# Block 1's attention on one Trainium2 core: a written TensorE order of head-set steps and dense pieces, key groups by turns, joined output banks

## The chip, the core and the metric

The kernel runs on one core of a Trainium2 chip. The metric is the device time of one execution in microseconds (us). TensorE (PE) multiplies; VectorE (DVE), ScalarE (ACT) and GpSimd (POOL) do the rest; SyncE (SP) issues most of the weight loads. A TensorE product is a weight load (PEld) and a matmul (PE).

## The reference, cut to what matters

Two blocks of two layers each, over 256 tokens of width 1024, all in float32. Block 1, the one whose attention changes:

```
for l in range(2):                                   # block 1
    p  = x @ w_in[l]                                 # split into NSA, MLA and forgetting-attention (FOX) parts
    o_nsa = nsa_attention(...)    # 8 heads of 64 in 2 key groups of 4 heads; three branches (compressed, selected, window)
    o_mla = mla_attention(...)    # 4 heads, key width 96
    o_fox = fox_attention(...)    # 4 heads, key width 64, decay added to the scores
    merged = sum(sigmoid(x @ w_gate)[i] * (o_i @ w_br_i)) ; y = merged @ w_out
    x = layer_norm(a * x + y)
    x = layer_norm(a * x + memory_cross_attention(x, mem))   # 4 heads of 64, 256 memory rows
    x = layer_norm(a * x + square(relu(x @ w_up)) @ w_down)
```

Every attention is `softmax(q k^T * scale + bias) v` for two blocks of 128 queries (t = 0 and 1; causal, so t = 0 sees 128 keys and t = 1 sees 256). Block 2 has pooling, retention and an RWKV-7 recurrence. The kernel computes that recurrence in two chunks of 128 tokens with the inverse of a unit triangular matrix per head.

## The kernel before, in words

**Dense products.** Each float32 weight is loaded by SP (`raw`), cast by ACT to a high part (`hi`, L112), and DVE subtracts to get the low part (`lo`, L113); a few units take POOL for L113 instead. A product is three matmuls (L138, L139, L140) with those parts. DVE and ACT therefore work through a queue of weight splits between all else they do, each in its fixed order. Small attention products are plain float32: one such instruction in the program shows as two in the trace.

**Order.** The Tile framework's scheduler orders each engine's instructions. Inside `tc.manual_schedule(engines={PE})` TensorE keeps the written order. Before, that is used in block 2's recurrence only, whose parts `yield` between pieces of dense products (`others`).

**Block 1's attention.** `scores` (L252) makes four heads' scores of one key group: matmuls at L263 into bank `s`, then the bias and the row maximum on DVE (L271) and the exponential on ACT (L274). NSA's group g = 0 has its keys and queries in rows 0 to 63 of `kvT` and `nqT`, g = 1 in rows 64 to 127; one call uses one half of the rows. `transposed` scales the weights by DVE and transposes them on TensorE (L295) into `PT`. `pv_pair` (L307) makes one pair of heads' outputs, 128x128, in a bank `o` of its own and splits it for the next product. `attend_nsa(t, g)` does both branches of one group; `attend_mla`, `attend_fox` and `attend_compressed` the rest. The scheduler lays these between the dense products of chunks 3 and 4 of `w_in` and of the gates (`gate_tanh`).

**Memory cross attention.** `Norm.finish` ends the layer norm (L338, L340 on DVE over `xr`, L343 the transposes), then come keys, query, `memory_scores`, `memory_values`, `memory_weights`, `attend_memory`, and the output product. The low parts of the key and query weights are made on POOL.

**Block 2's inverse.** The 16x16 diagonal blocks are inverted on DVE; the inverse and its transpose go to two DRAM scratch tensors, `zd` and `td`, on POOL's DMA queue (L1112, L1111) in pieces of 64 bytes, and come back block-diagonal as `TT` and `Tn` (L1122). `invert` starts with `Tn` (L1130). At the same time SP loads the weights of the retention part, on which ACT's cast and DVE's split, and behind them L1292 (`kT`) and the products L1339, depend.

Of the kernel before, what the change touches and what calls it, by code (L numbers as in the profile page):

```python
# [42 lines left out]
def program(ctx: ExitStack, tc: tile.TileContext, T: dict, out: bass.AP):  # L43
# [208 lines left out]
    def scores(nk, qk, addm):  # L252

        P = bt("P", [128, 4, 256], F32, 4)
        hb = 512 // nk
        sums = st("sums", [128, 4])
        nmx = st("nmx", [128, 4])
        for b in range(0, 4, hb):
            p = pst("s")
            pv = p[:, :hb * nk].rearrange("p (h k) -> p h k", k=nk)  # L260
            for i in range(hb):
                q, k = qk(b + i)
                pe.matmul(pv[:, i, :], lhsT=q, rhs=k, start=True, stop=True)  # L263
            if addm is None:
                src, sign = pv, 1.0
                ver.tensor_reduce(out=nmx[:, b:b + hb], in_=src, axis=AX.X, op=ALU.max, negate=True)
            else:
                src, sign = P[:, b:b + hb, :nk], -1.0
                am = addm(b, hb)
                for i in range(hb):  # L270
                    ver.tensor_tensor_reduce(out=src[:, i, :], in0=pv[:, i, :], in1=am[:, i, :], scale=-1.0,  # L271
                                             scalar=3e38, op0=ALU.add, op1=ALU.min, accum_out=nmx[:, b + i:b + i + 1])
            for i in range(hb):
                act.activation(out=P[:, b + i, :nk], in_=src[:, i, :], func=AF.Exp, bias=nmx[:, b + i:b + i + 1],  # L274
                               scale=sign, accum_out=sums[:, b + i:b + i + 1])
        return P, sums

# [8 lines left out]

    def transposed(P, sc, nk, tags=("t", "t")):

        res = []
        for kt in range(nk // 128):  # L290
            Pk = P[:, :, 128 * kt:128 * kt + 128]
            ver.tensor_mul(out=Pk, in0=Pk, in1=sc.unsqueeze(2).broadcast_to([128, 4, 128]))
            p = pst(tags[kt])
            for h in range(4):
                pe.transpose(p[:, 128 * h:128 * h + 128], Pk[:, h, :], ident)  # L295
            pt = bt("PT", [128, 4, 128], F32, 4)
            evac(pt.rearrange("p a b -> p (a b)"), p)
            res.append(pt)
        return res

    def pv_pair(dst, ki, t, terms):

        o = pst("o")
        both = list(zip(terms(0), terms(1)))
        for i, pair in enumerate(both):
            for half, (v, pt) in enumerate(pair):
                pe.matmul(o[64 * half:64 * half + 64, :128], lhsT=v, rhs=pt, start=i == 0, stop=i == len(both) - 1)  # L307
        h, l = dst.k(ki)
        s = slice(128 * t, 128 * t + 128)
        split_op(h[:, s], l[:, s], o[:, :128])  # L310

    class Norm:
# [18 lines left out]
        def finish(self, t):  # L331
            mv = st("mv", [128, 2])
            ver.bn_aggr(out=mv, in_=self.stats[t])
            r = rsqrt(mv[:, 1:2], LN_EPS)
            for i in range(2):
# [4 lines left out]
                ver.scalar_tensor_tensor(out=z, in0=z, scalar=r, in1=self.b[:, s], op0=ALU.mult, op1=ALU.add)  # L340
                p = pst("s" if self.op else ("s", "s", "t", "o")[2 * t + i])
# [38 lines left out]
    def block1_layer(l, x, xop, us, K):  # L380
# [210 lines left out]
        def attend_compressed(t):  # L591
# [17 lines left out]
            ver.tensor_mul(out=pcs, in0=pcs, in1=valid_c[:, t, :].unsqueeze(1).broadcast_to([128, 8, 16]))  # L609
            p = pst("t")  # L610
# [4 lines left out]
        def attend_nsa(t, g):  # L615
            nk = 128 * (t + 1)
            pts = []
            for br in range(2):
                kt_ = kvT[64 * g:64 * g + 64, 2 + br, 0:nk]
                b0 = 0 if t else 128  # L620
                P, sums = scores(nk, lambda h: (nqT[64 * g:64 * g + 64, h, tok(t)], kt_),
                                 lambda b, n: bias[:, 4 * g + b:4 * g + b + n, b0:b0 + nk])
                sc = st("sc", [128, 4])
                ver.reciprocal(out=sc, in_=sums)
                ver.tensor_mul(out=sc, in0=sc, in1=gates(t)[:, 4 * g:4 * g + 4, 1 + br])
                pts.append(transposed(P, sc, nk))

            for pr in range(2):
                def terms(half):
                    r = 2 * pr + half  # L630
                    res = [(vz[:, 4 * g + r, :], pct[t])]
                    for br in range(2):
                        for kt in range(t + 1):
                            res.append((vv[:, kt, 128 * br + 64 * g:128 * br + 64 * g + 64], pts[br][kt][:, r, :]))
                    return res
                pv_pair(oop, 2 * g + pr, t, terms)

        def attend(t, k0, qT, kT, vt, v0, kr):
            nk = 128 * (t + 1)
            tm = tri_bias[:, (0 if t else 128):256]  # L640
            P, sums = scores(nk, lambda h: (qT[0:kr, h, tok(t)], kT[0:kr, h, 0:nk]),
                             lambda b, n: tm.unsqueeze(1).broadcast_to([128, n, nk]))
            sc = st("sc", [128, 4])
            ver.reciprocal(out=sc, in_=sums)
            pt = transposed(P, sc, nk)
            for pr in range(2):
                pv_pair(oop, k0 + pr, t,
                        lambda half: [(vt[:, kt, v0 + 128 * pr + 64 * half:v0 + 128 * pr + 64 * half + 64],
                                       pt[kt][:, 2 * pr + half, :]) for kt in range(t + 1)])

        attend_mla = lambda t: attend(t, 4, mq, mk, mv, 0, 96)
        attend_fox = lambda t: attend(t, 6, fqT, fkT, vv, 256, 66)

        def gate_tanh(c, br):
            us = pairs(T["w_gate"][l], 8 * br + 4 * c)
            tt = bt("gt", [128, 4, 256], F32, 4)
            for j in range(0, 4, 2):
                p = pst("mm")
                for i in range(2):
                    gemm_b(p[:, 256 * i:256 * i + 256], xop, us, 128 * (j + i))  # L660
                act.activation(out=flat2(tt[:, j:j + 2, :]), in_=p, func=AF.Tanh, scale=0.5)
            return tt

        if first:
            turn()
        attend_mla(0)
        us = chunk(3)
        o = [pst("mm"), pst("mm")]
        gemm_a(o, xop, us)
        for t in range(2):  # L670
            evac(vv[:, t, :], o[t])
        attend_compressed(0)
        attend_mla(1)
        us = chunk_b(4)
        for j in range(4):
            p = pst("mm")
            gemm_b(p[:, 0:256], xop, us, 128 * j)
            for i in range(2):
                if j < 2:
                    act.activation(out=fqT[0:64, 2 * j + i, :], in_=p[64 * i:64 * i + 64, 0:256],  # L680
                                   func=AF.Copy, scale=0.125)
                else:
                    ver.tensor_copy(out=fkT[0:64, 2 * (j - 2) + i, :], in_=p[64 * i:64 * i + 64, 0:256])
        if x is None:
            x = load_x()
        th = {}
        attend_nsa(0, 0)
        th[0, 0] = gate_tanh(0, 0)
        attend_fox(0)
        attend_nsa(0, 1)  # L690
        attend_compressed(1)
        th[0, 1] = gate_tanh(0, 1)
        attend_nsa(1, 0)
        attend_fox(1)
        attend_nsa(1, 1)
        th[0, 2] = gate_tanh(0, 2)
        th[1, 0] = gate_tanh(1, 0)

        mop = new_op(8, "P", 4)
        for c in range(2):  # L700
            for br in range(3):
                if (c, br) not in th:
                    th[c, br] = gate_tanh(c, br)
# [30 lines left out]
        def memory_values():  # L734
            us = [unit(T["xa_kv"][l, 2 + i], 256, 4) for i in range(2)]
            o = [pst("mm"), pst("mm")]
            gemm_a(o, memop, us, n=256)
            for t in range(2):
                act.copy(out=xakv[:, 1, t], in_=o[t][:, :256])
# [7 lines left out]
        def memory_scores(t):  # L747
            return scores(256, lambda i: (xq[64 * (i // 2):64 * (i // 2) + 64, i % 2, tok(t)],
                                          xakv[64 * (i // 2):64 * (i // 2) + 64, 0, i % 2, :]), None)

        def memory_weights(P, sums):
            sc = st("sc", [128, 4])
            ver.reciprocal(out=sc, in_=sums)
            return transposed(P, sc, 256, ("s", "t"))

        def attend_memory(t, pt):
            for pr in range(2):
# [146 lines left out]
    def block2_layer(l, x, r, us, K, xop):  # L904
# [211 lines left out]
        def inverse_parts():  # L1116

            Tn = [bt("Tn", [128, 8, 64]) for n in range(2)]
            for n in range(2):
                for d, t in ((K["td"], Tn[n]), (K["zd"], TT[n])):  # L1120
                    for a in range(2):
                        pool.dma_start(out=t[half(a)], in_=flat(d, 16 + 8 * HS * n + 64 * 129 * a, [128, 64], [HS, 8], [1, 64]))  # L1122
# [685 lines left out]
```

## Time and profile before

| what | value |
|---|---|
| median of 3 runs | 1672.89 us (1668.97 to 1673.03) |
| profiled execution | 1675.49 us, its span 1673.6 us |
| TensorE busy | 95% of the span |
| DVE, ACT, POOL busy | 66%, 44%, 17% |
| granted TensorE clock, mean | 0.973 |

The span is the part of the execution that the trace covers; 1.9 us lie outside it. A TensorE row of the timeline shows start, duration and count; durations overlap the next instruction, so the price of a group is the distance to the start of the next row.

### The profile page before, as it was taken

To read this page: it belongs to the slowest core of one execution; us is meant where nothing else is said; L and a number is where in the kernel's file an instruction comes from. 1 tells how busy PE (TensorE), PEld (TensorE's weight loads), DVE (VectorE), ACT (ScalarE), POOL (GpSimd) and SP (SyncE) were. 2 spreads that over 40 slices of the span, in tenths; PEclk is the share of its full clock that TensorE was granted. 3 is DMA by queue.
4 is the path that set the end of the run, shared out by engine and by line. 5 is a ranking of instruction groups with operands and counts; after the bars stand their busy time and mean duration, and the time that the engine had idled before them with its cause. 6 is when DMAs were issued, how large, how long until landed. Compare 5 with 4: busy or idle time off the path is not lost. (4 is left out here: it accounts for less than half of the span.)

```text
span 1673.6 us, 29627 instructions
## 1 busy us (share of the span) xinstructions
PE 1588.1 (95%) x11978; PEld 1442.6 (86%) x11978; DVE 1104.7 (66%) x1801; ACT 742.7 (44%) x1212; POOL 280.1 (17%) x266
## 2 busy tenths in 40 slices
PE   7999998999999999998999989889999999699998
PEld 6787997798878888986989879879999889699997
DVE  5557567876776665678966677665556677555654
ACT  4655444454445654444544364323443643233441
POOL 1000112111100000231201132401111313201202
PEclk9899999999999999999999979989999989899999
DMA  8732466487776333663777835643355345533552
GB/s 295 265 127 76 139 206 209 139 282 263 266 252 208 101 102 102 199 204 124 252 247 264 280 105 170 160 129 114 113 187 180 102 139 167 152 105 112 175 179 74
DMA packets 81752, 291.34 MB, mean 174 GB/s; under 512 B 9400, under 2 KB 10496, under 8 KB 81616
## 3 DMA queue, kind: packets, MB, share of 16 engines
q1 hardware_dynamic: 78768, 280.07, 50.8%
q0 software_dynamic: 2848, 9.39, 2.2%
q8 instruction: 94, 1.54, 0.4%
q14 instruction: 42, 0.34, 0.1%
HBM read 282.52 MB, written 6.88 MB: 173 GB/s over the span
## 5 line engine op out<-in xcount | busy, mean ns | idle before, releaser
L113 DVE TENSOR_TENSOR lo<-raw,hi 128x1024 fp32r<-128x1024 f32 (+1 forms) x421 | 532.8, 1272 | 282.1 <-ACT hi L112 280.5
L112 ACT CAST hi<-raw 128x1024 fp32r<-128x1024 f32 (+1 forms) x435 | 452.7, 1048 | 581.5 <-PE mm L139 242.6
L138 PE MATMUL mm<-act,hi 128*128 128x256 f32 x1808 | 523.3, 290 | 2.0 <-DVE act L130 2.0
L139 PE MATMUL mm<-act,hi 128*128 128x256 f32 x1808 | 520.0, 288 | 0.0
L140 PE MATMUL mm<-act,lo 128*128 128x256 f32 x1808 | 518.9, 287 | 0.0
L138 PEld LDWEIGHTS mm<-act,hi 128*128 128x128 f32 x1808 | 351.4, 194 | 7.2 <-issue 2.7
L139 PEld LDWEIGHTS mm<-act,hi 128*128 128x128 f32 x1808 | 351.0, 194 | 4.7 <-issue 4.3
L140 PEld LDWEIGHTS mm<-act,lo 128*128 128x128 f32 x1808 | 350.7, 194 | 2.6 <-issue 2.3
L138 PE MATMUL s<-act,hi 128*128 128x256 f32 x448 | 128.2, 286 | 6.9 <-ACT PT L834 4.3
L138 PE MATMUL mm<-hi,act 128*128 128x512 f32 (+1 forms) x320 | 125.1, 392 | 5.5 <-ACT hi L127 4.9
L140 PE MATMUL s<-act,lo 128*128 128x256 f32 x448 | 127.6, 285 | 0.0
L139 PE MATMUL s<-act,hi 128*128 128x256 f32 x448 | 127.6, 285 | 0.0
L139 PE MATMUL mm<-lo,act 128*128 128x512 f32 (+1 forms) x320 | 123.6, 386 | 0.8 <-DVE lo L113 0.8
L140 PE MATMUL mm<-hi,act 128*128 128x512 f32 (+1 forms) x320 | 123.2, 385 | 0.0
L138 PEld LDWEIGHTS s<-act,hi 128*128 128x128 f32 x448 | 86.8, 194 | 8.3 <-ACT PT L834 4.9
L139 PEld LDWEIGHTS s<-act,hi 128*128 128x128 f32 x448 | 86.7, 194 | 0.2
L140 PEld LDWEIGHTS s<-act,lo 128*128 128x128 f32 x448 | 86.8, 194 | 0.0
L839 POOL TENSOR_TENSOR PT<-PT 128x512 f32<-128x512 f32 x28 | 38.6, 1378 | 241.2 <-ACT P L838 115.1
L138 PEld LDWEIGHTS mm<-hi,act 128*128 128x128 f32 x320 | 60.9, 190 | 19.5 <-ACT hi L127 4.9
L1545 DVE CUSTOM_DVE_ANT_0 raw<-raw,gt 128x1024 f32<-128x1024 f32 x48 | 59.9, 1250 | 26.0 <-DMA raw<-in_w_ada 25.9
L138 PE MATMUL mm<-hi,P 128*128 128x512 f32 x192 | 74.8, 390 | 0.0
L139 PE MATMUL mm<-lo,P 128*128 128x512 f32 x192 | 74.8, 390 | 0.0
(486 smaller groups left out, 2418.2 us busy)
## 6 DMA issues: line engine op xcount, KB each, us to landing
raw<-in_w_in SPq DMA_DIRECT2D x119, 512.0 KB, 4.8
raw<-in_w_up SPq DMA_DIRECT2D x64, 512.0 KB, 4.7
raw<-in_w_down SPq DMA_DIRECT2D x64, 512.0 KB, 4.7
raw<-in_w_gate SPq DMA_DIRECT2D x48, 512.0 KB, 3.3
raw<-in_w_ada SPq DMA_DIRECT2D x48, 512.0 KB, 4.7
raw<-in_w_gl SPq DMA_DIRECT2D x48, 512.0 KB, 3.5
raw<-in_w_branch SPq DMA_DIRECT2D x24, 512.0 KB, 3.4
raw<-in_w_br SPq DMA_DIRECT2D x16, 512.0 KB, 3.3
```

The lines of the kernel that those rows point to most:

```text
L112: act.copy(out=h[:, :cols], in_=r[:, :cols])
L113: (eng or ver).tensor_sub(out=l[:, :cols], in0=r[:, :cols], in1=h.bitcast(F32)[:, :cols])
L138: pe.matmul(o, lhsT=lh, rhs=rh, start=first, stop=False)
L139: pe.matmul(o, lhsT=lh, rhs=rl, start=False, stop=False)
L140: pe.matmul(o, lhsT=ll, rhs=rh, start=False, stop=last)
L839: pool.tensor_mul(out=r, in0=r, in1=r)
L1545: ver.tensor_tensor_reduce(out=r, in0=r, in1=box["c"], scale=1.0, scalar=0.0, op0=ALU.mult, op1=ALU.add, accum_out=mods[l][:, o:o + 1])
```

## The change

Three parts.

1. **Attention of block 1.** A class `Scores` takes one set of heads or two; with two (NSA's two key groups) it writes their matmuls by turns into two banks. `attend_nsa(t, br)` now does one branch of both groups; it accumulates all four output pairs of a t over both branches in one bank `o`, which one split reads. `attend` (MLA, FOX) joins its two pairs in one bank too. The whole is in a manual schedule: every job is a generator that yields after its scores, its transposes and its products, and a table of 22 slots says which job takes a step before which of the 24 dense pieces (12 matmuls of 512 columns, or 24 of 256).
2. **Memory cross attention.** The scores alternate halves of the rows, both t stand back to back, and the rest follows in a written order; the output bank is joined. The four low parts that POOL made go to DVE.
3. **Block 2's inverse.** `td` and its copy, write and four reads go; `Tn` is made on TensorE as the product of `TT` with the identity. This adds a `yield`, so the dense pieces that go with the recurrence come one step earlier.

The core of the diff:

```diff
+        def add(self, b, n):
+            nk = self.nk
+            hb = 512 // nk
+            banks = [[pst("s") for _ in range(0, n, hb)] for _ in self.sets]
+            at = lambda k, i: banks[k][i // hb][:, nk * (i % hb):nk * (i % hb) + nk]
+            for i in range(n):
+                for k, (qk, _) in enumerate(self.sets):
+                    q, kt = qk(b + i)
+                    pe.matmul(at(k, i), lhsT=q, rhs=kt, start=True, stop=True)
...
-        def attend_nsa(t, g):
+        acc = [None, None]
+        def attend_nsa(t, br):
...
+            for b in range(0, 4, 512 // nk):
+                sc.add(b, 512 // nk)
+                yield
+            sc.weigh(lambda g: gates(t)[:, 4 * g:4 * g + 4, 1 + br])
+            pts = yield from sc.transposed()
+            yield
+            if br == 0:
+                acc[t] = pst("o")
...
+        with tc.manual_schedule(engines={mybir.EngineType.PE}):
...
+            pieces = dense()
+            for slot in ("m0", "c0", "m1", "m0 c0", "m0 00", "m1 c1", "m1 01", "00 c1", "00 f0", "01 10", "01 10", "f0",
+                         "f0 f1", "10", "10", "10 11", "11", "f1", "f1", "11", "11", "11"):
+                for n in slot.split():
...
+                    next(jobs[n], None)
+                next(pieces, None)
...
-        us_k = [unit(T["xa_kv"][l, i], 256, 4, pool) for i in range(2)]
-        us = [unit(T["xa_q"][l, i], 256, 4, pool) for i in range(2)]
+        us_k = [unit(T["xa_kv"][l, i], 256, 4) for i in range(2)]
+        us = [unit(T["xa_q"][l, i], 256, 4) for i in range(2)]
...
-        pool.dma_start(out=flat(K["td"], 1, *blocks), in_=tb)
         pool.dma_start(out=flat(K["zd"], 16, *blocks), in_=zrow)
...
+            Tn = [bt("Tn", [128, 8, 64]) for n in range(2)]
+            for n in range(2):
+                p = pst("to"[n])
+                product(p, of(TT[n]), lambda i, a: ident[half(a), half(a)])
+                evac(flat2(Tn[n]), p)
+            yield
```

**TensorE, the first NSA scores of layer 0** (t = 0; `s` the score banks, `kvT`, `nqT` keys and queries of both groups). Before, with dense products around them:

```order
L263 MATMUL s_1277<-kvT_206,nqT_463 128x128 x4
L138 MATMUL mm_1392<-act_87,hi_1369 128x256
L139 MATMUL mm_1392<-act_88,hi_1369 128x256
L140 MATMUL mm_1392<-act_87,lo_1370 128x256
L263 MATMUL s_1304<-kvT_206,nqT_463 128x128 [waits DVE_49]
L263 MATMUL s_1304<-kvT_206,nqT_463 128x128 x3
L138 MATMUL mm_1392<-act_87,hi_1369 128x256
```

Now:

```order
L675 MATMUL mm_864<-PT_844,mv_679 64x128 x3
L270 MATMUL s_877<-kvT_205,nqT_462 128x128 [waits DVE_49]
L270 MATMUL s_878<-kvT_205,nqT_462 128x128 [waits DVE_49]
L270 MATMUL s_877<-kvT_205,nqT_462 128x128
L270 MATMUL s_878<-kvT_205,nqT_462 128x128
L270 MATMUL s_877<-kvT_205,nqT_462 128x128
L270 MATMUL s_878<-kvT_205,nqT_462 128x128
L270 MATMUL s_877<-kvT_205,nqT_462 128x128
L270 MATMUL s_878<-kvT_205,nqT_462 128x128
L138 MATMUL mm_927<-act_86,hi_905 128x256 [waits PE_49]
```

The two key groups stand by turns in two banks, and one dense piece of 24 products follows undivided. Over the attention of layer 0 the order goes from small work into dense products 44 times before, 23 times now.

**DVE, the first layer norm ahead of memory attention in layer 0** (`xr` the normalized tokens, `lo` low parts). Before:

```order
L328 SCALAR_TENSOR_TENSOR xr_1037<-xr_1037,mm_2650 128x512 [waits PE_49]
L329 BN_STATS bn_2545<-xr_1037 128x6 [waits DVE_49]
L333 BN_AGGR mv_2738<-bn_2545 128x2 [waits DVE_49]
L172 TENSOR_SCALAR rs_2740<-mv_2738 128x1 [waits DVE_49]
L338 SCALAR_TENSOR_TENSOR xr_1037<-xr_1037,mv_2738,gt_2700 128x512 [waits DMAHW0_49]
L338 SCALAR_TENSOR_TENSOR xr_1037<-xr_1037,mv_2738,gt_2700 128x512
L340 SCALAR_TENSOR_TENSOR xr_1037<-xr_1037,rs_2742,gt_2702 128x512 [waits DMAHW1_49,DVE_49,Pool_49]
```

Now (L347 and L349 are L338 and L340 of before):

```order
L342 BN_AGGR mv_2704<-bn_2511 128x2 [waits DVE_49]
L172 TENSOR_SCALAR rs_2706<-mv_2704 128x1 [waits DVE_49]
L347 SCALAR_TENSOR_TENSOR xr_1171<-xr_1171,mv_2704,gt_2666 128x512 [waits DMAHW0_49]
L347 SCALAR_TENSOR_TENSOR xr_1171<-xr_1171,mv_2704,gt_2666 128x512
L113 TENSOR_TENSOR lo_2693<-raw_2690,hi_2692 128x1024 [waits DMAHW6_49,Activation_49]
L113 TENSOR_TENSOR lo_2699<-raw_2696,hi_2698 128x1024 [waits DMAHW7_49,Activation_49]
L349 SCALAR_TENSOR_TENSOR xr_1171<-xr_1171,rs_2708,gt_2668 128x512 [waits DMAHW1_49,DVE_49,Pool_49]
```

Two low parts that POOL made now stand between the two steps of the norm; the other two stand a few rows earlier.

**TensorE, the start of block 2's inverse in layer 0** (`Tn` the diagonal inverses, `TT` their transposes, `LT` the triangle, `cpack` holds the identity). Before:

```order
L1354 MATMUL mm_11022<-gt_10766,gt_10996 128x128
L1130 MATMUL t_11051<-Tn_10843,LT_10371 64x64 [waits DMASW1_49]
L1130 MATMUL t_11051<-Tn_10843,LT_10371 64x64 [waits DMASW2_49]
L1130 MATMUL t_11051<-Tn_10843,LT_10371 64x64 x14
L1130 MATMUL o_11070<-Tn_10844,P_10372 64x64 [waits DMASW4_49]
L1130 MATMUL o_11070<-Tn_10844,P_10372 64x64 [waits DMASW5_49]
L1130 MATMUL o_11070<-Tn_10844,P_10372 64x64 x14
L138 MATMUL mm_11114<-hi_11091,act_9967 128x512 [waits PE_49,Activation_49]
```

Now:

```order
L1432 MATMUL mm_10939<-gt_10689,gt_10913 128x128
L1202 MATMUL t_10970<-cpack,TT_10370 64x64 [waits DMASW6_49]
L1202 MATMUL t_10970<-cpack,TT_10370 64x64 [waits DMASW7_49]
L1202 MATMUL t_10970<-cpack,TT_10370 64x64 x14
L1202 MATMUL o_10988<-cpack,TT_10371 64x64 [waits DMASW0_49]
L1202 MATMUL o_10988<-cpack,TT_10371 64x64 [waits DMASW1_49]
L1202 MATMUL o_10988<-cpack,TT_10371 64x64 x14
L138 MATMUL mm_11031<-hi_11008,act_9893 128x512 [waits PE_49,Activation_49]
```

The inverse waits for `TT` instead of `Tn` and has 32 more products (64 instructions of the trace), ahead of the first dense piece. At the other end of the recurrence, between its last product L1186 and the transposes L1265 (now L1264 and L1343), 54 dense matmuls stood before and 30 stand now.

## Rows read from the trace of the kernel before

**Rows 1.** Windows, layer 0: length; PE, PEld, DVE, ACT, POOL busy; clock; DMA.

```profile
73.60:179.60 106.00, 106.00 (x778) 87.52 (x778) 65.77 (x198) 58.63 (x162) 3.22 (x6) 0.98 0.29 96
239.90:324.80 84.90, 77.32 (x466) 64.27 (x464) 69.03 (x96) 36.65 (x60) 19.02 (x12) 0.98 0.53 171
```

**Rows 2.** Groups and one source line in the attention stage of layer 0.

```profile
L295 PE MATMUL t<-cpack,P 128*128 128x128 f32 x72 | 11.3, 279 | 0.0
L307 PE MATMUL o<-PT,vv 128*64 128x128 f32 x120 | 10.9, 285 | 0.0
L263 PE MATMUL s<-kvT,nqT x64: 271/375/481, 107.5 to 165.7; 64*128 64x128 f32 x32, 64*128 64x256 f32 x32
```

**Rows 3.** Timeline of PE, attention stage: start, duration, instruction.

```profile
91.01 1.97 PE L263 MATMUL s<-mk,mq 96*128 96x256 f32 x8
92.63 0.47 PE L138 MATMUL mm<-act,hi 128*128 128x256 f32 x1
...
107.46 2.05 PE L263 MATMUL s<-kvT,nqT 64*128 64x128 f32 x16
...
156.23 0.70 PE L263 MATMUL s<-kvT,nqT 64*128 64x256 f32 x2
156.85 0.66 PE L295 MATMUL t<-cpack,P 128*128 128x128 f32 x4
157.26 0.36 PE L138 MATMUL mm<-act,hi 128*128 128x256 f32 x1
157.47 0.28 PE L139 MATMUL mm<-act,hi 128*128 128x256 f32 x1
157.58 0.29 PE L140 MATMUL mm<-act,lo 128*128 128x256 f32 x1
...
158.66 0.66 PE L295 MATMUL t<-cpack,P 128*128 128x128 f32 x4
159.25 0.44 PE L307 MATMUL o<-PT,vv 128*64 128x128 f32 x4
159.62 1.13 PE L263 MATMUL s<-kvT,nqT 64*128 64x256 f32 x4
...
163.17 1.04 PE L307 MATMUL o<-PT,vv 128*64 128x128 f32 x16
```

**Rows 4.** Timeline of PE, block 2's masked scores, whose halves alternate.

```profile
1028.14 1.16 PE L1075 MATMUL s<-Ee,Bt 64*128 64x128 f32 x16 [0.38 <-DVE Bt L1058]
```

**Rows 5.** Timelines of DVE and POOL in the memory stage of layer 0.

```profile
259.52 5.63 DVE L340 SCALAR_TENSOR_TENSOR xr<-xr,rs,gt 128x512 f32<-128x512 f32 x2
...
269.21 1.41 DVE L340 SCALAR_TENSOR_TENSOR xr<-xr,rs,gt 128x512 f32<-128x512 f32 x2
...
259.37 5.24 POOL L113 TENSOR_TENSOR lo<-raw,hi 128x1024 fp32r<-128x1024 f32 x2
```

**Rows 6.** DVE's weight splits, the page's costliest groups.

```profile
L113 DVE TENSOR_TENSOR lo<-raw,hi 128x1024 fp32r<-128x1024 f32 (+1 forms) x421 | 532.8, 1272 | 282.1 <-ACT hi L112 280.5
```

**Rows 7.** PE's waits: total us, times, longest.

```profile
PE mm L1339 <- DVE kT L1292: 16.6, 2, 9.8
...
PE t L1265 <- DVE PT L1258: 4.1, 2, 2.0
```

**Rows 8.** DMA issues from 1040 to 1100 us: count, KB, us to landing.

```profile
raw<-in_w_in SPq DMA_DIRECT2D x16, 512.0 KB, 5.6
...
zd<-PT POOLq DMA_DIRECT2D x1, 128.0 KB, 9.1
td<-dg POOLq DMA_DIRECT2D x1, 128.0 KB, 11.7
```

**Rows 9.** Timeline of ACT, block 2 layer 0, during those transfers.

```profile
1080.33 1.04 ACT L112 CAST hi<-raw 128x1024 fp32r<-128x1024 f32 x1 [8.09 <-DMA raw<-in_w_in]
```

**Rows 10.** Timeline of PE, the inverse's first products.

```profile
1100.88 1.15 PE L1130 MATMUL t<-Tn,LT 64*64 64x64 f32 x32
1101.86 1.10 PE L1130 MATMUL o<-Tn,P 64*64 64x64 f32 x32
```

More of the change, by code (lines that the diff above doesn't have):

```diff
@@ L250, in split_into @@
         split_op(flat2(h), flat2(l), r)
[L252 to L276, printed above, removed]
@@ L285, in evac @@
             ver.tensor_copy(out=o, in_=i)
[L287 to L310, printed above, removed]
     class Norm:
@@ L613, in attend_compressed @@
             act.copy(out=pct[t], in_=p[:, :128])
-        def attend_nsa(t, g):
+        acc = [None, None]
+        def attend_nsa(t, br):
             nk = 128 * (t + 1)
[L617 to L636, printed above, removed]
+            b0 = 0 if t else 128
+            rows = lambda g: slice(64 * g, 64 * g + 64)
+            sc = Scores(nk, [(lambda h, g=g: (nqT[rows(g), h, tok(t)], kvT[rows(g), 2 + br, 0:nk]),
+                              lambda h, g=g: bias[:, 4 * g + h, b0:b0 + nk]) for g in range(2)])
+            for b in range(0, 4, 512 // nk):
[3 more added lines that the diff above has]
+            pts = yield from sc.transposed()
+            yield
+            if br == 0:
+                acc[t] = pst("o")
+            for i in range(4):
+                g, pr = divmod(i, 2)
+                terms = [[] if br else [(vz[:, 4 * g + 2 * pr + half, :], pct[t])] for half in range(2)]
+                for half in range(2):
+                    for kt in range(t + 1):
+                        c = 128 * br + 64 * g
+                        terms[half].append((vv[:, kt, c:c + 64], pts[g][kt][:, 2 * pr + half, :]))
+                for k, pair in enumerate(zip(*terms)):
+                    for half, (v, pt) in enumerate(pair):
+                        pe.matmul(acc[t][64 * half:64 * half + 64, 128 * i:128 * i + 128], lhsT=v, rhs=pt,
+                                  start=br == i == k == 0, stop=br == 1 and i == 3 and k == t, skip_group_check=True)
+            if br:
+                h, lo = oop.parts[0]
+                split_op(h[:, :, tok(t)], lo[:, :, tok(t)], acc[t].rearrange("p (a b) -> p a b", b=128))
@@ L640, in attend, with gate_tanh @@
             tm = tri_bias[:, (0 if t else 128):256]
[L641 to L645, printed above, removed]
-            for pr in range(2):
[L647 to L654, printed above, removed]
+            sc = Scores(nk, [(lambda h: (qT[0:kr, h, tok(t)], kT[0:kr, h, 0:nk]), lambda h: tm)])
+            sc.add(0, 4)
+            yield
+            sc.weigh()
+            pt, = yield from sc.transposed()
+            yield
+            p = pst("mm")
+            for pr in range(2):
+                for kt in range(t + 1):
+                    for half in range(2):
+                        c = v0 + 128 * pr + 64 * half
+                        pe.matmul(p[64 * half:64 * half + 64, 128 * pr:128 * pr + 128], lhsT=vt[:, kt, c:c + 64],
+                                  rhs=pt[kt][:, 2 * pr + half, :], start=kt == 0, stop=kt == t)
+            h, lo = oop.parts[1]
+            split_op(h[:, k0:k0 + 2, tok(t)], lo[:, k0:k0 + 2, tok(t)], p[:, 0:256].rearrange("p (a b) -> p a b", b=128))
+        attend_mla = lambda t: attend(t, 0, mq, mk, mv, 0, 96)
+        attend_fox = lambda t: attend(t, 2, fqT, fkT, vv, 256, 66)
+        def gate_tanh(tt, c, br):
             us = pairs(T["w_gate"][l], 8 * br + 4 * c)
-            tt = bt("gt", [128, 4, 256], F32, 4)
             for j in range(0, 4, 2):
@@ L660, in gate_tanh @@
                     gemm_b(p[:, 256 * i:256 * i + 256], xop, us, 128 * (j + i))
+                    yield
                 act.activation(out=flat2(tt[:, j:j + 2, :]), in_=p, func=AF.Tanh, scale=0.5)
[L662 to L674, printed above, removed]
@@ L686, in block1_layer, with dense @@
-        th = {}
[L687 to L697, printed above, removed]
+        th = {}
+        xs = [x]
+        def dense():
+            us = chunk(3)
+            o = [pst("mm"), pst("mm")]
+            for i in range(4):
+                gemm_a(o, xop, us[i:i + 1], k0=2 * i, first=i == 0, last=i == 3)
+                if i == 3:
+                    for t in range(2):
+                        evac(vv[:, t, :], o[t])
+                yield
+            us = chunk_b(4)
+            for j in range(4):
+                p = pst("mm")
+                gemm_b(p[:, 0:256], xop, us, 128 * j)
+                for i in range(2):
+                    if j < 2:
+                        act.activation(out=fqT[0:64, 2 * j + i, :], in_=p[64 * i:64 * i + 64, 0:256],
+                                       func=AF.Copy, scale=0.125)
+                    else:
+                        ver.tensor_copy(out=fkT[0:64, 2 * (j - 2) + i, :], in_=p[64 * i:64 * i + 64, 0:256])
+                yield
+            if x is None:
+                xs[0] = load_x()
+            for c, br in ((0, 0), (0, 1), (0, 2), (1, 0)):
+                th[c, br] = bt("gt", [128, 4, 256], F32, 4)
+                yield from gate_tanh(th[c, br], c, br)
@@ new lines, in block1_layer @@
+        with tc.manual_schedule(engines={mybir.EngineType.PE}):
+            if first:
+                turn()
+            job = {"m": attend_mla, "f": attend_fox, "c": attend_compressed}
+            jobs = {}
+            pieces = dense()
+            for slot in ("m0", "c0", "m1", "m0 c0", "m0 00", "m1 c1", "m1 01", "00 c1", "00 f0", "01 10", "01 10", "f0",
+                         "f0 f1", "10", "10", "10 11", "11", "f1", "f1", "11", "11", "11"):
+                for n in slot.split():
+                    if n not in jobs:
+                        jobs[n] = job[n[0]](int(n[1])) if n[0] in job else attend_nsa(int(n[0]), int(n[1]))
+                    next(jobs[n], None)
+                next(pieces, None)
+            for _ in pieces:
+                pass
@@ L747, in memory_scores @@
         def memory_scores(t):
-            return scores(256, lambda i: (xq[64 * (i // 2):64 * (i // 2) + 64, i % 2, tok(t)],
-                                          xakv[64 * (i // 2):64 * (i // 2) + 64, 0, i % 2, :]), None)
-        def memory_weights(P, sums):
+            ps_ = [pst("s" if t == 0 else "mm") for _ in range(2)]
+            for i in range(2):
+                for g, p in enumerate(ps_):
+                    pe.matmul(p[:, 256 * i:256 * i + 256], lhsT=xq[64 * g:64 * g + 64, i, tok(t)],
+                              rhs=xakv[64 * g:64 * g + 64, 0, i, :], start=True, stop=True)
@@ L1438, in block2_layer @@
             others = other_branches(on)
-            for _ in recurrence(Tn):
+            for _ in recurrence():
                 next(others, None)
```

163 lines of the change are left out of this document (113 added, 50 removed).

## The prediction

> **What bounds the kernel now.** I first read the busy time by windows. In the attention stage of layer 0 TensorE is busy in all 106.0 us, with DVE at 65.8, ACT at 58.6 and the DMA share at 0.29 [rows 1]: the stage lasts as long as TensorE's instructions take to go through, so what is saved there in TensorE time comes off the end, as long as DVE and ACT keep up. In the memory stage TensorE is busy 77.3 of 84.9 us [rows 1]; 7.6 us are idle, and there the chain through DVE counts. Then the chain of waits: the longest one of TensorE anywhere is L1339 on `kT`, 16.6 us in two times, one for each layer of block 2 [rows 7]. Last the timelines of these three places, for the price of one instruction alone, in a run, and broken up by others [rows 3, 4]. I count from one start to the next where the next row stands, since durations overlap.
>
> **The change part by part.** All prices are for one layer and counted twice, since both layers of a block run the same instructions.
>
> *Scores of NSA.* There are 32 instructions of 64x128 and 32 of 64x256 in a layer [rows 2]. The narrow ones stood in runs on one half of the rows: 16 in 2.05 us, 128 ns each [rows 3]. The nearest thing to the new order is block 2's masked scores, same form, but with the halves by turns: 16 in 1.16, 73 ns, or 0.57 of that [rows 4]. So 32 x (128 - 73) = 1.8 us are saved. The wide ones stood mostly in twos: 0.62 for 2 between 156.23 and 156.85, 310 ns each; a run on one half takes 1.62 for 8 between 91.01 and 92.63, 203 ns [rows 3]. For before I take 280 ns, near the broken price, so 9.0 us in all. No row shows alternating halves at this width; 0.57 of 203 is 115 ns, 3.7 us, and 5.3 saved. Bounds: at no overlap at all 203 ns and 128 ns stay, and 9.0 - 6.5 = 2.5 us is saved in total, by the shorter queue alone; at a full half, 101 ns, it is 7.6. I take 7.1, since the narrow row shows the overlap in this program.
>
> The Trainium skill, "TensorEngine Tiling (Array Packing)", Tiling Modes, Key Properties, says that tiles on different rows run in parallel, and in Overview, Theoretical Speedup, that a contraction of at most 64 can gain up to twofold. The rows give 1.77, not 2; by the page's limit this term would be 7.6, an estimate of half a microsecond more than mine.
>
> *Output products.* 120 instructions of one form [rows 2] and 56 like them (by the code, the compressed and MLA values), 176. They cost 92 ns in a run of four (0.37 from 159.25 to 159.62), 65 in a run of 16 (1.04) [rows 3]. Before they stood in both ways, I take 80; now they stand in runs of 8 to 32, I take 65. Saved: 176 x 15 ns = 2.6 us; bounds 0 and 4.8.
>
> *Transposes.* 72 [rows 2]; four take 0.59 or 0.41 us, the first from 158.66, the other from 156.85 [rows 3]. In runs of up to 16 I take 0.40 for four against 0.46 as a mix of both: 1.1 us saved, bounds 0 and 3.4.
>
> *Breaks in the dense products.* A dense product takes 0.11 us inside a run (157.47 to 157.58), and 0.21 as the first after small work (157.26 to 157.47) [rows 3]. Of the last one before small work I take the same 0.10 more. The order enters dense work 44 times before and 23 now: 21 x 0.2 = 4.2 us, and 2.1 if only the first product pays.
>
> The same page, Key Properties, says that a change of tiling mode drains TensorE. That speaks against the change, since each slot now goes through scores, transposes, products and dense work, but the number of such changes falls too, and the row's 0.10 us is that drain's size if the page is right.
>
> *Joined banks and weighing.* Fewer evictions and one multiply for each set make DVE's and ACT's load smaller. TensorE is the bound, so I count nothing; the cover is that DVE is busy 65.8 of 106 us and of some 92 after.
>
> *What the written order costs.* TensorE now stops at an instruction that isn't ready, with all dense pieces behind it, where the scheduler's order had something else ready. Chains have three or more slots of about 4 us from scores to transposes, one slot from transposes to products. DVE needs 65.8/22 = 3.0 us a slot for all its work, splits of 1.27 us each [rows 6] included. I take 1 us a layer; from below 0, from above by the rival below. **Attention: 7.1 + 2.6 + 1.1 + 4.2 - 1.0 = 14 us a layer, 28 in all.**
>
> *Memory stage.* The last step of the norm, L340, takes 5.63 us for two while POOL makes two low parts in 5.24, and 1.41 for two without that [rows 5]. The move to DVE gives back 4.2 and puts two splits of 1.27 [rows 6] between L338 and L340: 1.7 us gained, on the path to the transposes, keys and query. The two earlier splits go into DVE's queue ahead of the last addition of the norm; the product that this waits for covers them. If it doesn't, they cost 2.5, and the sum is 0.9 worse than before. Sixteen score instructions by turns save 16 x (203 - 115) ns = 1.4. Together 3 us a layer; bounds 0.9 lost and, with all 7.6 us of idle gone, 7.6 gained. **6 in all.**
>
> *Block 2's inverse.* The two writes in small pieces take 9.1 and 11.7 us to land, `Tn`'s reads come behind them, and in that time weight loads, 5.6 us otherwise, come so late that ACT sits idle for 8.09 before one cast [rows 8, 9]. DVE's splits stand in order behind the casts, `kT` behind the splits, and L1339 behind `kT` [rows 7]. `td` is half of these writes, and its four reads are half of the reads. I take it that the two waits at L1339 go, 16.6 us; bound below 0, if `zd` alone holds up the loads as long.
>
> The Trainium skill, "DMA: Bandwidth & Descriptors", Why small descriptors are slow, says that each small piece to or from HBM carries a fixed overhead. The 9.1 and 11.7 us for 128 KB agree.
>
> Against that stand 64 instructions of 64x64 a layer, 32 of which take 0.98 us from 1100.88 to 1101.86 [rows 10]: 2.0 us, with nothing beside them on TensorE. And there are 24 dense products fewer between the recurrence's last product and L1265, 24 x 0.12 = 2.9 us less cover. TensorE waits there already, 4.1 us in two times [rows 7], so the whole 2.9 shows, and the wait becomes about 5 us. **16.6 - 2 x 4.9 = 7 in all**; bounds 10 lost and, if the end is covered, 13 gained.
>
> **Sum.** 28 + 6 + 7 = 41 us. The profiled execution took 1675.5, 1.9 outside its span and 2.6 over the median; 1675.5 - 41 = 1634.5, and as a median 1632.
>
> **The rivals.**
>
> *No overlap at either width.* The narrow row speaks against it, that no row has the wide form for it. Attention then saves 4.6 less a layer: 1641.
>
> *The written order waits.* What speaks for it: DVE and ACT work in order, with splits of 1.27 us ahead of a chain's step, and the FOX scores of t = 0 come right behind the copies of their keys. Against it: three slots of distance. At 0.5 us a slot, 22 slots, two layers, 22 us are lost: 1654.
>
> *The other side.* The same wait, but where a chain stays behind once it is late: at 41/44 = 0.93 us a slot the gain is used up, and at 1.5 us the time is 1632 + 66 = 1698. The point from which it decides is that DVE's work of a slot, 3.0 us, plus two splits in the wrong place, 2.5, exceeds the slot's 4.1.
>
> *`zd` alone holds the loads.* The page gives 9.1 us for it with `td` beside it, so how long it takes alone isn't seen. Then 16.6 aren't saved and 9.8 are paid: 1649.
>
> *More than I count.* Memory stage without idle, wide scores at a half, longer runs: 41 + 9 + 1 + 8, about 1614.
>
> **How the numbers follow.** I give my forecast 0.46 (its own range 1618 to 1647, from the half of each bound), no overlap 0.12, waits at half a microsecond 0.12, `zd` 0.13, more than counted 0.08, the other side 0.09. A measurement of this kernel tells 0.3%, 5 us, from no change. All but the last lie below 1668: faster 0.90; of the last, 0.03 within 5 us of 1673 and 0.07 above. The range 1612 to 1660 holds all cases but the last and the outer ends of the others.
>
> **What would show each step.** The attention stage of layer 0 lasts about 92 us, with 64x256 scores by turns at about 115 ns each and dense pieces of 24 in about 2.9 us. TensorE's idle time in it stays under 2 us; over 10 would make the prediction wrong. L349 takes about 0.7 us each. The wait at the place of L1339 is gone or small, ACT's idle of 8 us too, and the wait at L1343 (L1265 of before) is about 5 us. If the time is above 1660, I expect waits of TensorE in the slots, or L1339's wait as before.

## The result, and the profile after

The changed kernel takes 1627.64 us (median of 4 runs, 1626.35 to 1632.15), the one before 1672.96 in the same comparison. The ratio is 0.9734, 95% interval 0.9705 to 0.9762: 45 us faster, 2.7%. The prediction said 1632, with 1612 to 1660 as its range. The profiled execution took 1626.35 us, its span 1624.6.

The page's busy time after, engine by engine:

```profile
PE 1555.3 (96%) x12106; PEld 1433.0 (88%) x12106; DVE 1104.6 (68%) x1773; ACT 741.3 (46%) x1190; POOL 252.3 (16%) x247
```

TensorE has 128 instructions more, the identity products, and still 33 us less busy time than the 1588.1 of before. DVE's busy time is the same to 0.1 us.

The stages, first of before, then of after: windows with length, busy time of PE, PEld, DVE, ACT and POOL, granted clock, DMA share and GB/s. Two stretches each for attention with the gates, for memory attention, and for block 2 from its retention's first products to the end of the recurrence:

```profile
73.60:239.90 166.30, 166.30 (x1280) 147.82 (x1281) 101.35 (x236) 84.38 (x191) 13.57 (x12) 0.99 0.38 126
543.60:708.95 165.35, 165.29 (x1279) 146.79 (x1280) 101.23 (x236) 84.23 (x191) 11.46 (x8) 1.00 0.38 123
...
708.95:795.54 86.59, 78.47 (x467) 65.44 (x465) 72.42 (x107) 38.60 (x64) 20.92 (x15) 0.96 0.52 170
1011.80:1199.70 187.90, 170.86 (x1628) 159.20 (x1627) 119.18 (x223) 63.62 (x102) 44.20 (x54) 0.97 0.47 136
1342.10:1549.60 207.50, 189.99 (x1723) 176.20 (x1723) 130.96 (x234) 71.74 (x113) 44.06 (x51) 0.94 0.46 138
```

```profile
72.70:227.60 154.90, 152.93 (x1281) 143.01 (x1282) 99.18 (x221) 82.98 (x181) 13.61 (x12) 0.99 0.42 138
526.50:679.80 153.30, 151.36 (x1281) 142.54 (x1282) 99.16 (x221) 82.82 (x181) 11.46 (x8) 1.00 0.40 132
227.60:309.20 81.60, 74.83 (x467) 63.40 (x465) 70.92 (x99) 37.27 (x59) 10.60 (x8) 1.00 0.54 187
679.80:764.45 84.65, 76.41 (x466) 64.52 (x464) 74.72 (x112) 40.24 (x65) 12.22 (x11) 0.98 0.57 183
976.40:1160.40 184.00, 173.65 (x1693) 161.85 (x1692) 119.67 (x223) 64.86 (x103) 40.35 (x49) 0.98 0.44 135
1302.30:1499.10 196.80, 186.82 (x1787) 173.94 (x1787) 133.46 (x235) 73.05 (x114) 39.02 (x46) 0.98 0.46 143
```

Layer 0's memory stage of before stands in [rows 1]. Attention is shorter by 11.4 and 12.1 us, memory attention by 3.3 and 1.9, block 2 by 3.9 and 10.7: 43.3 of the 49.0 us between the two spans. The rest lies in stretches whose instructions are the same; the profiled execution of before was 2.6 us above its median and this one 1.3 below, which may be 3.9 of those 5.7. The granted clock of the attention windows is the same before and after (0.99 and 1.00); in the other four windows it is 0.01 to 0.04 higher after.

How that looks in the attention of layer 0, on TensorE's timeline (start, duration, instruction, count, idle time before it):

```profile
93.07 1.16 PE L270 MATMUL s<-kvT,nqT 64*128 64x128 f32 x16
94.16 0.38 PE L138 MATMUL mm<-act,hi 128*128 128x256 f32 x1
94.38 0.28 PE L139 MATMUL mm<-act,hi 128*128 128x256 f32 x1
...
97.13 0.60 PE L302 MATMUL t<-cpack,P 128*128 128x128 f32 x4
97.57 0.60 PE L302 MATMUL mm<-cpack,P 128*128 128x128 f32 x4
...
107.39 0.60 PE L302 MATMUL mm<-cpack,P 128*128 128x128 f32 x4
109.20 0.33 PE L625 MATMUL t<-cpack,pcs 128*128 128x128 f32 x1 [1.21 <-DVE PT L315]
...
119.06 1.14 PE L270 MATMUL s<-kvT,nqT 64*128 64x256 f32 x8
120.12 0.39 PE L138 MATMUL mm<-act,hi 128*128 128x256 f32 x1
...
170.85 1.97 PE L655 MATMUL o<-PT,vv 128*64 128x128 f32 x32
172.75 0.39 PE L138 MATMUL mm<-act,hi 128*128 128x256 f32 x1
```

From start to start, sixteen narrow scores take 1.09 us, 68 ns each, and eight wide ones 1.06, 133 ns; before it was 1.98 for sixteen (107.46 to 109.44; the 2.05 of [rows 3] is the duration) and 0.62 for two. Output products take 59 ns in their longest run (1.90 for 32). The first dense product after scores takes 0.22, as before. Apart from the first MLA scores, which wait 0.74 us for their keys, the one wait inside the slots is at L625, 1.21 us.

TensorE's longest waits that bear on the change (total us, times, longest):

```profile
PE mm L1417 <- DVE kT L1370: 8.9, 2, 5.1
...
PE t L1343 <- DVE PT L1336: 3.9, 2, 1.9
...
PE t L625 <- DVE PT L315: 2.4, 2, 1.2
```

L1417 is L1339 of before: 16.6 us became 8.9, not nothing. L1343 is L1265: 4.1 became 3.9, where I had expected about 10 [rows 7]. Two waits beside the one for `kT` shrank too; before:

```profile
PE mm L1334 <- DVE gt L1322: 4.7, 2, 2.9
PE mm L1351 <- DVE gt L1336: 4.4, 2, 3.3
```

Their places are L1412 and L1429 now, with 0.2 and 2.2 us. ACT's idle time of 8.09 us ahead of a cast [rows 9] is 4.70 (before the cast at 1041.03). And DVE's norm ahead of memory attention, with the two splits between its steps:

```profile
247.28 2.35 DVE L113 TENSOR_TENSOR lo<-raw,hi 128x1024 fp32r<-128x1024 f32 x2
249.55 1.41 DVE L349 SCALAR_TENSOR_TENSOR xr<-xr,rs,gt 128x512 f32<-128x512 f32 x2
```

3.7 us for what took 5.63 without splits [rows 5]. TensorE's waits for `xr` in this window, 3.0 us before, are gone, but others stand in their place (1.5 us at L140, 1.5 at L892). Its idle time went from 7.6 to 6.8 us in layer 0's window and from 8.1 to 8.2 in layer 1's. So most of the 3.3 and 1.9 us is TensorE's own busy time, 2.5 and 2.1 less, at a granted clock 0.02 higher.

### The profile page after: what moved, and what is told of

Read it like the earlier page. It is cut to its first block, busy times and chain, and to the rows that moved or that the text cites. A ratio compares the mean times of both kernels' runs of the same rounds, so it can differ in the third digit from the quotient of the medians.

```text
span 1624.6 us, 29823 instructions
## 1 busy us (share of the span) xinstructions
PE 1555.3 (96%) x12106; PEld 1433.0 (88%) x12106; DVE 1104.6 (68%) x1773; ACT 741.3 (46%) x1190; POOL 252.3 (16%) x247
## 4 chain that ended last, share of the span: by engine, by line
PE 42%; DVE 6%; DMA 2%; ACT 2%; issue 2%; POOL 1%; DVEq 0%; POOLq 0%; ACTq 0%
PE mm L138 10%; PE mm L139 10%; PE mm L140 10%; DVE lo L113 2%; PE s L138 2%; PE s L139 2%; PE s L140 2%; DMA raw<-in_w_in 1%; PE s L1154 1%; ACT hi L112 1%; PE o L1270 1%; PE t L1270 1%; PE o L1301 1%; PE t L1202 1%; PE s L1202 0%
## 5 line engine op out<-in xcount | busy, mean ns | idle before, releaser
L113 DVE TENSOR_TENSOR lo<-raw,hi 128x1024 fp32r<-128x1024 f32 (+1 forms) x429 | 545.6, 1279 | 258.1 <-ACT hi L112 256.1
L140 PE MATMUL mm<-act,lo 128*128 128x256 f32 x1808 | 513.6, 285 | 0.0
L140 PEld LDWEIGHTS mm<-act,lo 128*128 128x128 f32 x1808 | 347.7, 193 | 0.5 <-issue 0.2
L140 PE MATMUL s<-act,lo 128*128 128x256 f32 x448 | 127.5, 285 | 0.0
L140 PE MATMUL mm<-hi,act 128*128 128x512 f32 (+1 forms) x320 | 123.8, 387 | 3.0 <-DVE act L128 3.0
L140 PEld LDWEIGHTS s<-act,lo 128*128 128x128 f32 x448 | 86.7, 194 | 0.0
L138 PEld LDWEIGHTS mm<-hi,act 128*128 128x128 f32 x320 | 61.4, 192 | 18.1 <-ACT hi L127 5.2
L140 PEld LDWEIGHTS mm<-hi,act 128*128 128x128 f32 x320 | 61.2, 191 | 17.0 <-DVE act L128 4.3
```

The source lines that it names most:

```text
L113: (eng or ver).tensor_sub(out=l[:, :cols], in0=r[:, :cols], in1=h.bitcast(F32)[:, :cols])
L138: pe.matmul(o, lhsT=lh, rhs=rh, start=first, stop=False)
L140: pe.matmul(o, lhsT=ll, rhs=rh, start=False, stop=last)
```

## The experiments

Theory: three mechanisms, one in each part, that add up. Attention is shorter because TensorE's own instructions take less time, memory attention because POOL's splits no longer slow DVE's norm, block 2 because fewer small pieces delay its weight loads. Rivals: the gain comes from unbroken runs and not from halves side by side; the parts depend on each other; block 2 is faster only because of the order or because of the reads. Line numbers of the single-part kernels differ.

**One part at a time.** The kernel before with the hunks of one part.

> Block 1's attention alone (the class of scores, the slots, the joined banks), memory attention and block 2's inverse as before. If the three parts add, as the stages of the two traces say: two attention stages of about 11.7 us less each, 23 us less, about 1650 us. If the attention's gain is taken back by the old memory stage that follows it (its splits on POOL and DVE not ready earlier), under 15 us less, above 1658.

Measured: 1645.47 us, ratio 0.9851 (0.9820 to 0.9883).

> Memory cross attention alone (scores by turns, written order, joined bank, the four low parts from POOL to DVE). If the parts add: 3.4 us less in layer 0 and about 0.5 to 4 in layer 1, 4 to 7 us less, about 1667. If the moved splits only take DVE's time from the norm and the rest is due to the attention before it, 0 to 2 us less.

Measured: 1666.90 us, ratio 0.9982 (0.9967 to 0.9997).

> Block 2's inverse alone. If the parts add: about 4 us less in layer 0 and 7 to 10 in layer 1, 11 to 15 us less, about 1660, with the wait at the place of L1339 near 9 us in two times instead of 16.6. If the loads come earlier only because the whole program before is shorter, no change of that wait, and up to 5 us slower by the identity products.

Measured: 1658.57 us, ratio 0.9933 (0.9907 to 0.9959). Its longest wait of TensorE:

```profile
PE mm L1338 <- DVE kT L1291: 9.9, 2, 5.0
```

Attention alone gives 1.5%, the inverse 0.7%, memory 0.2%: 2.3% together, against 2.7% (2.4 to 3.0) for the whole. Within the intervals the parts add. Attention alone is at the expected 23 us or a little above, so the old memory stage takes nothing back. The wait at `kT` falls in the inverse alone as it does in the whole. Memory's 3 us is the least sure: less than the trace's 5 us, and its interval almost touches no change.

**Are the halves side by side, and does the turn matter?** First the turn:

```diff
-            for i in range(n):
-                for k, (qk, _) in enumerate(self.sets):
+            for k, (qk, _) in enumerate(self.sets):
+                for i in range(n):
                     q, kt = qk(b + i)
```

> The changed kernel, with the NSA scores of one key group all ahead of those of the other, in the same two banks and slots. If the two halves of the rows run side by side: 64x128 at about 124 ns and 64x256 at about 203 ns each instead of 68 and 133, 4 us more in each layer, 8 in all, about 1635. If the gain comes from unbroken runs alone: no change, about 1628.

Measured: 1634.25 us (1626.84 to 1635.88), ratio 0.9765 (0.9729 to 0.9801), so the time tells little. Its timeline does:

```profile
92.36 1.71 PE L270 MATMUL s<-kvT,nqT 64*128 64x128 f32 x16
94.00 0.38 PE L138 MATMUL mm<-act,hi 128*128 128x256 f32 x1
...
119.23 1.14 PE L270 MATMUL s<-kvT,nqT 64*128 64x256 f32 x8
120.30 0.39 PE L138 MATMUL mm<-act,hi 128*128 128x256 f32 x1
```

Neither expectation holds. The narrow run takes 1.64 instead of 1.09, 102 ns each, between 68 and 124. The wide run takes 1.07 as before. Four wide instructions of one half followed by four of the other cost the same as eight by turns; eight narrow ones followed by eight don't. The two cases differ in width as well as in number. By these rows the edit costs 1.1 us a layer; the other 7 us of this profiled span came in stretches that the edit doesn't touch.

Then both groups on the same half:

```diff
-            rows = lambda g: slice(64 * g, 64 * g + 64)
+            rows = lambda g: slice(0, 64)
```

> The changed kernel, in which both key groups of NSA read the rows 0 to 63, so group 1 computes with group 0's queries and keys; all instructions, banks and the order stay. If two halves of the rows run side by side: 64x128 goes from 68 to about 124 ns each, 64x256 from 133 to about 203, 4 us more in each attention stage. If only the unbroken runs of eight and sixteen count: no change of the rows.

Measured: 1641.77 us, 14 more than the changed kernel. The timeline:

```profile
90.40 2.05 PE L270 MATMUL s<-kvT,nqT 64*128 64x128 f32 x16
92.38 0.38 PE L138 MATMUL mm<-act,hi 128*128 128x256 f32 x1
...
117.77 1.99 PE L270 MATMUL s<-kvT,nqT 64*128 64x256 f32 x8
119.69 0.38 PE L138 MATMUL mm<-act,hi 128*128 128x256 f32 x1
```

1.98 us for sixteen and 1.92 for eight: 124 and 240 ns against 68 and 133. Only which rows are read has changed, so the halves do run side by side, 1.8 times as fast at both widths. "TensorEngine Tiling (Array Packing)" of the Trainium skill, Overview, Theoretical Speedup, has up to twofold for this; the rows agree, a little short of it. In a layer that is 32 x 107 ns for the wide and 32 x 56 ns for the narrow ones, 5.2 us; two layers make 10.4 of the 14 us. The rest of the attention's gain was not taken apart by a run; it stands on the sum of rows further down.

**The new yield.** My prediction charged it with 2.9 us a layer.

```diff
                 evac(flat2(Tn[n]), p)
-            yield
```

> The changed kernel without the new yield behind the products that make Tn, so the dense pieces stand beside the recurrence as before the change. By my prediction's step, the missing 24 products at the recurrence's end cost 2.9 us a layer, so this is about 5 us faster at that end (the wait there as long as now, 1.9 us, is 2.9 us shorter in all). By the trace after, the splits that the last dense piece releases go with it into the chain on DVE: the end gets no shorter, and the products behind Tn wait for its eviction, 1 to 2 us a layer: 0 to 4 us slower.

Measured: 1629.07 us, ratio 0.9744 (0.9718 to 0.9769), no difference that the runs can tell. Why my step fails is seen on DVE between the recurrence's last product and the transposes; first without the yield, then the changed kernel:

```profile
1149.29 0.41 DVE L1329 TENSOR_TENSOR PT<-o,ymu 128x256 f32<-128x256 f32 x1
1150.67 1.23 DVE L113 TENSOR_TENSOR lo<-raw,hi 128x1024 fp32r<-128x1024 f32 x1 [0.97 <-ACT hi L112]
1151.82 0.74 DVE L1333 TENSOR_REDUCE yvr<-dg 128x4 f32<-128x256 f32 x2
1152.47 0.29 DVE L172 TENSOR_SCALAR rs<-yvr 128x4 f32<-128x4 f32 x2
1152.72 1.23 DVE L113 TENSOR_TENSOR lo<-raw,hi 128x1024 fp32r<-128x1024 f32 x1
1154.85 0.43 DVE L1335 TENSOR_TENSOR PT<-PT,rs 128x256 f32<-128x256 f32 x1 [0.90 <-POOL rs L174]
```

```profile
1155.88 0.41 DVE L1330 TENSOR_TENSOR PT<-o,ymu 128x256 f32<-128x256 f32 x1
1156.51 0.75 DVE L1334 TENSOR_REDUCE yvr<-dg 128x4 f32<-128x256 f32 x2 [0.21 <-ACT dg L1332]
1157.17 0.29 DVE L172 TENSOR_SCALAR rs<-yvr 128x4 f32<-128x4 f32 x2
1158.46 0.43 DVE L1336 TENSOR_TENSOR PT<-PT,rs 128x256 f32<-128x256 f32 x1 [1.00 <-POOL rs L174]
```

Without the yield, two weight splits stand in the norm's chain, from 1149.29 to 1154.85 5.6 us; with it the same chain takes 2.6. The dense piece that moved takes the splits that come with it along. TensorE has 24 products less to do there and waits as long, 1.9 us. In the two traces the stretch from the identity products to L1343 is 1.1 us longer without the yield in each layer, since TensorE then waits 1.2 us for `Tn`'s eviction. So the yield is worth about 1 us a layer and costs nothing.

**td's write alone.**

```diff
+        tb = bt("dg", [128, 16, 16])
+        ver.tensor_copy(out=tb, in_=bass.AP(...))
+        pool.dma_start(out=flat(K["td"], 1, *blocks), in_=tb)
         pool.dma_start(out=flat(K["zd"], 16, *blocks), in_=zrow)
```

> The changed kernel with the copy and the write of td put back (2048 pieces of 64 bytes a layer on POOL's queue), which nobody reads. If the small writes hold up the weight loads: the wait at L1417 goes from 8.9 us in two times back to 13 to 17, 5 to 10 us slower. If td's reads did it: no change of that wait.

Measured: 1637.98 us, ratio 0.9793 (0.9769 to 0.9818), 10 us slower than the changed kernel. Its longest waits:

```profile
PE mm L1421 <- DVE kT L1374: 8.3, 2, 4.3
PE mm L1416 <- DVE gt L1404: 6.1, 2, 3.1
```

The time is as the write's theory said, the place isn't: the wait for `kT` (L1421 here) stays near 8.9, and the loss comes one step earlier, at the place of L1412. By the sign set beforehand, no change of that wait, the reads would have done it; but one wait alone tells too little. The stretch of 620 TensorE instructions up to the inverse's first product tells more; in layer 1 of the kernel before, of this run and of the changed kernel (length, busy times, granted clock, DMA share, GB/s):

```profile
1348.94:1450.72 101.78, 87.36 (x621) 81.92 (x621) 69.88 (x115) 40.28 (x64) 27.69 (x32) 0.92 0.59 169
...
1309.70:1407.32 97.62, 87.61 (x622) 81.81 (x621) 69.39 (x115) 40.30 (x64) 23.89 (x28) 0.92 0.60 179
...
1306.05:1398.18 92.13, 85.34 (x622) 80.24 (x621) 72.01 (x116) 40.25 (x64) 23.14 (x27) 0.96 0.62 187
```

Both layers together, it takes 200.4, 193.3 and 184.3 us. A write that nobody reads thus costs 9 of the 16 us that `td`'s removal gave here, and 10 in the time. The other 7 went with its four reads or with what the removal changed in the order; no run separates these.

**What zd still costs.** Without its write and reads:

```diff
-        pool.dma_start(out=flat(K["zd"], 16, *blocks), in_=zrow)
...
-                    pool.dma_start(out=TT[n][half(a)], in_=flat(K["zd"], ...))
+                pool.tensor_copy(out=flat2(TT[n])[:, 0:256], in_=flat2(zrow))
+                pool.tensor_copy(out=flat2(TT[n])[:, 256:512], in_=flat2(zrow))
```

> The changed kernel without the write of zd and its four reads in block 2; TT is filled by copies on POOL, so the inverse has other numbers and the same instructions. If zd's small pieces still hold up the weight loads as td's did: the waits at L1412 and L1417, 8.9 us at L1417 alone, fall under 4 us, and the time is 8 to 12 us less, about 1618. If what is left there is the loads' own rate: the waits stay within 2 us.

Measured: 1619.15 us (1618.05 to 1620.24), 8.5 less. The wait for `kT` is down to 0.7 us; what is left in this place is

```profile
PE mm L1428 <- DVE gt L1413: 5.3, 4, 1.8
```

The stretch up to the inverse's first product takes 175.1 us in both layers, with a granted clock of 1.00 for the changed kernel's 0.96; in layer 1:

```profile
1302.06:1389.87 87.81, 83.14 (x622) 77.96 (x621) 71.15 (x115) 40.26 (x64) 24.19 (x26) 1.00 0.58 186
```

So the remaining write with its four reads costs 7 to 9 us: 8.5 by the medians, 7 by the ratios to the kernel before, 9 in the stretch. It is a limit and no version to use, since the inverse needs these values.

**The splits on POOL.** `pool` put back in the two lines of the diff.

> The changed kernel with the four low parts of the memory keys and queries on POOL again. If POOL's split beside DVE's norm is what slows L349: two L349 take 5 us or more instead of 1.41, and the memory stage is 1.7 us longer in layer 0, 3 to 4 us in both. If it was the order alone: no change.

Measured: 1629.50 us, ratio 0.9753 (0.9733 to 0.9774), which tells no difference. The rows do:

```profile
246.38 5.63 DVE L349 SCALAR_TENSOR_TENSOR xr<-xr,rs,gt 128x512 f32<-128x512 f32 x2
...
246.22 5.23 POOL L113 TENSOR_TENSOR lo<-raw,hi 128x1024 fp32r<-128x1024 f32 x2
```

DVE's two steps take 5.63 again, with POOL's two splits beside them almost from start to end. The Trainium skill, "SBUF — State Buffer", SBUF: two separate sides, says that a DVE instruction with two inputs there and a POOL instruction share a port pair that one holds for its whole length while the other is blocked; the rows agree, 5.63 beside 5.23 and 1.41 without. The memory scores of layer 0 begin 2.7 us later against the changed kernel, of which 1.6 are left at the end of the layer. So the mechanism is there, and what it is worth in the time of the kernel is less than these runs can tell.

**A version that moves one step.**

```diff
-            for slot in ("m0", "c0", "m1", "m0 c0", "m0 00", "m1 c1", "m1 01", "00 c1", "00 f0", "01 10", ...
+            for slot in ("m0", "c0", "m1", "m0 c0", "m0 00", "m1 c1", "m1 01", "00", "00 f0 c1", "01 10", ...
```

> The changed kernel with one entry of the slot table moved: the second step of the compressed branch of t = 1 (one transpose into a bank t) comes in the ninth slot, behind the products of the slot, instead of in the eighth, right behind the eight transposes whose eviction frees its bank. If that eviction is what TensorE waits for there: the wait at L625, 2.4 us in two times, goes, and the time is 2 us less, about 1625. If the wait only moves to the next step in the slot: no change.

Measured: 1626.02 us (1623.44 to 1630.10), ratio 0.9742 (0.9719 to 0.9764). The wait at L625 is gone, and the slots behind it come 1.6 and 1.5 us earlier in the two layers. That is under what the runs can tell. Of the versions here that compute everything I would keep this one, for the wait that is gone from its trace and not for its time.

## Why the prediction was right

The sum, 41 us for 45, is nearer than its parts. Attention gave 23.5 us in the traces where I had 28, memory 5.2 where I had 6, block 2 14.6 where I had 7; that these partly cancel is luck. Another 5.7 us of the two spans lie in stretches that the change leaves as they were.

*Attention, predicted 14 us a layer, measured 11.4 and 12.1.* The mechanism was right: the stage was TensorE's own time. Its terms, summed from start to start over layer 0's rows: scores 6.6 saved (predicted 7.1), products 3.4 (2.6), transposes 0.4 (1.1), dense work 3.5 (4.2), and waits of 2.0 lost (1.0). The scores' price at the wide form, the one I had no row for, was 133 ns and not 115; I scaled by 0.57 from a run at 203 whose form is another (96 rows), where the same half costs 240. The ratio held (133/240 is 0.55), its base didn't. A run of the right form on one half stood in the trace of before:

```profile
145.12 1.99 PE L263 MATMUL s<-kvT,nqT 64*128 64x256 f32 x8
```

The next instruction starts at 147.04, so these eight cost 240 ns each. Of the 32 wide ones only 12 stood in twos; the average of all was 277 ns, so the 280 for before was right and the price after was not. Of the breaks, I charged 0.10 us to the last dense product ahead of any small work. Its price (256 columns) in the trace of before is 0.21 instead of 0.12 us ahead of products with 64 rows or 64 columns, but mostly 0.12 ahead of transposes. The first dense product takes 0.20 or 0.21 us behind transposes too, which use all 128 rows and columns; so no row shows that its 0.10 us is the drain of a tiling change. The stage up to its last small product took 100.0 us and not the 92 that I gave as a sign, with 46 instructions more in it than before; only the longer windows above compare the same work.

*The written order's waits.* I gave them 1 us a layer and a rival up to the whole gain. Measured: 2.0 us of idle in 154.9 (154.90 - 152.93 in the window), 1.2 of it one entry of the table and most of the rest the first MLA scores, which wait for their keys. Before, such scores waited 0.70 us just ahead of the window (at 73.58), so about 1.2 are new. The distance of three slots was enough everywhere else.

*Memory, predicted 3 a layer, measured 3.3 and 1.9 in the traces.* The step on L340 came out (5.63 became 2.35 and 1.41, a gain of 1.9 for 1.7), but little of it reached TensorE's idle time, as shown above. The scores' 1.4 us weren't there: the sixteen took 2.29 us before and 2.20 after, from start to start. The old order already had four of one half and then four of the other, which the wide run of the fourth experiment shows to be as good as turns; I had priced it by the 203 ns of another form. What the rest of the gain comes from isn't shown. Alone, the part gave 3 us in all.

*Block 2, predicted 7 in all, measured 14.6 in the traces and 11 alone.* 3.1 of the 14.6 lie at the start of layer 1's window, ahead of what this part changes: there the same work took 6.84 us at a granted clock of 0.50 before (1342.10 to 1348.94; the lower of the two levels, 1.2 GHz) and 3.74 at 1.00 after (1302.30 to 1306.04). TensorE had been busy 8.08 of 10 us in 1320 to 1330 before and 8.07 of 10 in 1280 to 1290 after, so why the clock fell in one trace alone isn't shown. The other 11.5, near the 11 alone, are 15.7 gained up to the inverse's first product and 4.2 lost behind it.

My term for the gain, 16.6, was right in size and wrong in place. I took the whole wait at L1339 as `td`'s; it gave 7.7, and the half that stayed is `zd`'s, by the run without it. The waits at L1334 and L1351, which I had left out, gave 6.7. That the two make up for each other is luck. The identity products cost what I took (2.1 us a layer behind the start of the inverse, for 2.0). The step that failed is the 5.8 us for shorter cover at L1343, which didn't come: "the whole 2.9 shows" counted what the moved piece covers and not what it brings with it, two splits in DVE's chain.

## What to carry to other kernels

Small products with 64 rows should read different halves in neighbouring instructions: here it gave 1.8 times the rate, and groups of four of the wide form did as well as single turns. When a dense piece moves, move in thought the weight splits that its end releases: here they decided the wait, not the cover. And price a small-piece write by leaving it out or adding it, since its own landing time says nothing of the loads that it delays: here a 128 KB write cost 5 us a layer. Look at the whole stretch then and not at one wait: the wait for `kT` stayed as it was when the write came back.

## What was not expected

Four wide scores on one half and then four on the other take 1.07 us, as eight by turns (1.06), while eight and eight narrow ones take 1.64 against 1.09. In these rows the overlap reaches over groups of four and only in part over groups of eight; where it ends, and whether the width matters, these runs don't tell.
